# Layer 1's second-half output projection on the MLP's PSUM ring, with eight load buffers for its mixed tiles

## The chip, the cores and the metric

One core of one Trainium2 chip runs the whole program, once per launch. The time is device time in microseconds, from one launch; smaller is better. The core has five instruction queues that matter here: TensorE (PE; its weight loads are listed as PEld), VectorE (DVE), ScalarE (ACT), GpSimd (POOL) and SyncE (SP), which issues the DMA transfers. Each queue works its instructions off in order. SBUF and PSUM have 128 partitions; PSUM has eight banks, each of 512 float32 values a partition.

## What is computed

A trunk of two layers on a sequence of 1024 tokens with 1024 features, in float32. Layer 0 mixes with a convolution and attention on a memory, layer 1 with three kinds of attention. Both end in the same way, and only this end of layer 1 matters here:

```python
def squared_relu_mlp(h, w_in, w_out):
    return jnp.square(jax.nn.relu(h @ w_in)) @ w_out

# in each layer l, after the mixing
x = x + mix @ w_out[l]                                   # w_out: 1024 x 1024
x = x + squared_relu_mlp(rms_norm(x, norm_mlp_g[l]), w_mlp_in[l], w_mlp_out[l])   # 1024 x 4096 x 1024
```

## The kernel before

Features lie on partitions and tokens in columns. The sequence is worked in two halves of 512 tokens, so that a tile is 128 features by 512 tokens; x, the mixed activations (`act`) and the output of a half are eight such tiles each (`KT` = 8). To keep float32 accuracy each operand is split into a high and a low part (`split`: ACT copies the high part, L88, DVE takes the difference, L89), and each product is three matmuls: high by high, high by low, low by high. A weight tile (`weight`, L101 to L110) is loaded by SP into a buffer tagged `raw` (L106), copied by ACT (L109) and its difference taken (L110) into a buffer tagged `hl`; for half 1's output projection L110 is on DVE, for the MLP on POOL.

The end of layer 1 is written at L1288 to L1302. `load_mix` (L376 to L381) loads the eight mixed tiles of a half from DRAM scratch (`mixd`, to which the attention has stored them) and splits them into `act`. `w_out` (L384 to L411) is the output projection: four pairs of output tiles (`ps_wo`), for each tile eight weight pieces of 128 x 128, held in two weight tiles, 48 matmuls a pair, 192 in all (L400 to L402); each finished tile is added to the residual (L404), squared on ACT, and added up in `acc` (L140). Then `act` is overwritten by x times the norm's gain, split again (L409, L410). `inv_rms` (L414 to L422) sums the squares over partitions (L150), makes the inverse root with small DVE operations, spreads it over all partitions with one more matmul (L164) and copies it with ACT to the tile `r` (L420). `mlp` (L424 to L473) does 16 rounds of an input projection of two tiles (`ps_i`, L441 to L443; scaled by `r` in L449, squared, split) and an output projection of eight tiles (`ps_mo`, L81 to L83), each of which is added to x by DVE (L463). The last round of a half stores x to the output (L1301 before the change, L1302 behind it).

Half 0 of this end (weights `k`, PSUM pool `ps2` with two banks) is written ahead of half 1 (context `ka`), but the order on the engines is made by a scheduler, which takes the instructions by priority and by when buffers come free: half 0's MLP runs in between the attention of half 1, and half 1's output projection follows on its last round. Buffers are given out by tag from pools; a tag with n buffers is a ring of n. A pool opened on the place of a closed one gives its first tile only when the readers of the old tiles there are done.

In the lines that the change touches, half 1's projection has a PSUM pool of its own, `psb`, with four banks (tag `a`), closed behind it; `ps3`, with four banks (tag `mm`), is opened when the MLP of half 1 is written, and stands on the same banks. The eight mixed tiles are loaded into the tag `raw`, three buffers (`NRAWA`), which also takes the weights.

Of the kernel before, what the change touches and what calls it, by code (L numbers as in the profile page):

```python
# [21 lines left out]
MIXORD = (4, 5, 6, 7, 0, 1, 2, 3)  # L22
# [64 lines left out]
def split(nc, hi, lo, src, eng=None):  # L87
    return (nc.scalar.activation(hi, src, AF.Copy),  # L88
            (eng or nc.vector).tensor_tensor(lo, src, hi.bitcast(F32), op=ALU.subtract))  # L89
# [286 lines left out]
def load_mix(k, act, src, kts, pool, tag="raw", bufs=2):  # L376

    for kt in kts:
        raw = pool.tile([P, HF], F32, tag=tag, name="mix", bufs=bufs)
        k.nc.sync.dma_start(raw, src[:, kt])  # L380
        split(k.nc, act[kt][:, 0], act[kt][:, 1], raw)  # L381


def w_out(k, l, mix, x, resid):  # L384


    nc = k.nc
    acc = k.tmp.tile([P, HF], F32, tag="acc", name="acc", bufs=2)
    for o in range(0, KT, WG):
        rs, ps = [], []  # L390
        for i in range(WG):
            rs.append(k.tmp.tile([P, HF], F32, tag="a", name="rs", bufs=2))
            nc.sync.dma_start(rs[i], resid[:, o + i])
            ps.append(k.psum.tile([P, HF], F32, tag=k.tag, name="ps_wo", bufs=k.nps))
        for g, kts in ((1, MIXORD[:4]), (0, MIXORD[4:])):
            w = [weights(k, k.i["w_out"][l, o + i][:, 512 * g:512 * g + 512], P) for i in range(WG)]
            for kt in kts:
                for i in range(WG):
                    wh, wl = (w[i][kt % 4][:, x] for x in range(2))
                    nc.tensor.matmul(ps[i], lhsT=wh, rhs=mix[kt][:, 0], start=kt == MIXORD[0], stop=False)  # L400
                    nc.tensor.matmul(ps[i], lhsT=wh, rhs=mix[kt][:, 1], start=False, stop=False)
                    nc.tensor.matmul(ps[i], lhsT=wl, rhs=mix[kt][:, 0], start=False, stop=kt == MIXORD[-1])  # L402
        for i in range(WG):
            nc.vector.tensor_add(x[o + i], ps[i], rs[i])  # L404
            sq_add(k, acc, x[o + i], o + i == 0, nc.vector if o + i > 5 else None)
        k.pe(24 * WG * HF / 2.4)
    for o in range(KT):
        a, g = mix[MIXORD[o]], k.cols[:, (C_MLP0, C_MLP1)[l] + o:][:, 0:1]
        nc.scalar.activation(a[:, 0], x[o], AF.Copy, scale=g)  # L409
        nc.vector.scalar_tensor_tensor(a[:, 1], x[o], g, a[:, 0].bitcast(F32), op0=ALU.mult, op1=ALU.subtract)  # L410
    return inv_rms(k, acc)  # L411
# [716 lines left out]
def build(tc, ins, out):  # L1128
    nc = tc.nc
    k = K()  # L1130
# [3 lines left out]
    def pool(es, name, side="left"):  # L1134
        return es.enter_context(tc.tile_pool(name=name, bufs=1, side=side))

    def psum_pool(name):
        return tc.tile_pool(name=name, bufs=1, space=bass.MemoryType.PSUM)

    with ExitStack() as es:  # L1140
# [15 lines left out]
        mixd = dram.tile([2, P, KT, HF], F32, name="mixd")  # L1156
# [10 lines left out]
        def act_tiles(hf):  # L1167
            return [ap.tile([P, 2, HF], F32R, tag=f"act{hf}{kt}", name=f"act{hf}{kt}", bufs=1) for kt in range(KT)]

        act = [act_tiles(hf) for hf in range(2)]  # L1170
# [72 lines left out]
        ka = K()  # L1243
# [44 lines left out]
        act = [act_tiles(hf) for hf in range(2)]  # L1288
# [1 line left out]
        load_mix(k, act[0], mixd[0], MIXORD, k.wpool, "raw", k.nraw)  # L1290
        rs = [w_out(k, 1, act[0], x[0], xs[0])]
        ka.rpool = pool(es, "rb", "right")
        with psum_pool("psb") as psb, tc.tile_pool(name="wb", bufs=1, side="right") as wb:
            ka.psum, ka.wpool, ka.tmp = psb, wb, wb
            load_mix(ka, act[1], mixd[1], MIXORD, ka.wpool, "raw", ka.nraw)
            rs.append(iter(list(w_out(ka, 1, act[1], x[1], xs[1]))))
        for hf in range(2):
            if hf == 1:
                k.psum = es.enter_context(psum_pool("ps3"))
                k.nps = 4  # L1300
            mlp(k, 1, x[hf], act[hf], rs[hf], lambda o: nc.sync.dma_start(out[hf, :, o], x[hf][o]))  # L1301
        k.flush()  # L1302

# [67 lines left out]
```

## Time and profile before

| what | us |
|---|---|
| median of 3 runs | 2467.85 |
| the runs | 2460.43, 2467.85, 2468.43 |
| the profiled execution, its time | 2460.16 |
| its span, from the first to the last instruction | 2458.4 |
| TensorE busy in the span | 2366.0 |
| last round of half 0's MLP ends, projection of half 1 starts | 2035.15, 2042.74 |
| projection ends, MLP of half 1 starts | 2090.07, 2100.68 |

The profile is of one execution. A timeline row gives the start, the time taken, the engine, line and operation, the tiles written and read, the count, and in brackets how long the engine was idle before it and what ended that. Matmuls overlap, so that the start of the next one, not the time of one, tells their pace.

### The profile page before, as it was taken

The numbers are of one execution on the slowest core, as the hardware profiler recorded it, in microseconds if no ns is written. First come the engines' busy times: TensorE is split into PE (matmuls) and PEld (weight loads), VectorE is DVE, ScalarE is ACT, GpSimd is POOL, SyncE is SP. The second block draws the span as 40 slices with busy tenths as digits, with TensorE's granted clock in tenths as the row PEclk, the third lists the DMA queues.
The fourth block names the chain that finished last, engine by engine and source line by source line (L and its number), as shares of the span: only waits on it lengthen the run. The fifth ranks groups of instructions, "written<-read, shape, count | busy, mean of one in ns | idle before, by whom it ended". The sixth has DMA issues, their size and how long they took to land.

```text
span 2458.4 us, 36789 instructions
## 1 busy us (share of the span) xinstructions
PE 2366.0 (96%) x12098; PEld 1995.2 (81%) x12098; DVE 1674.5 (68%) x3594; ACT 1293.9 (53%) x2938; POOL 1227.3 (50%) x1056
## 2 busy tenths in 40 slices
PE   7997999999988999999999999999999998899999
PEld 5786788888777988888887798888888886788887
DVE  7898587998678677877446866778777764333433
ACT  6565555333545467776334545676666653333332
POOL 2776643545633256565445325666565542344443
PEclk9998999999999999999999999999999999899999
DMA  6311433332444242322335434222221225233333
GB/s 215 100 48 57 137 103 102 96 98 91 138 124 150 83 124 82 87 86 83 116 103 170 149 99 131 80 70 66 76 86 59 70 75 178 65 98 95 95 95 103
DMA packets 157790, 250.87 MB, mean 102 GB/s; under 512 B 17696, under 2 KB 49056, under 8 KB 157088
## 3 DMA queue, kind: packets, MB, share of 16 engines
q1 hardware_dynamic: 157600, 248.52, 32.8%
q8 instruction: 96, 1.57, 0.3%
q14 instruction: 94, 0.77, 0.1%
HBM read 217.52 MB, written 20.45 MB: 97 GB/s over the span
## 4 chain that ended last, share of the span: by engine, by line
PE 63%; DVE 4%; DMA 2%; issue 2%; POOL 1%; ACT 1%; SPq 0%; ACTq 0%; POOLq 0%; DVEq 0%
PE ps_i L441 7%; PE ps_i L443 7%; PE ps_i L442 7%; PE ps_mo L81 6%; PE ps_mo L83 6%; PE ps_mo L82 6%; PE ps_t L1033 4%; PE ps_s L989 4%; PE ps_o L1049 2%; PE ps_o L1052 2%; PE ps_tok L666 1%; PE ps_tok L667 1%; PE ps_tok L668 1%; PE ps_wo L400 1%; PE ps_wo L402 1%
## 5 line engine op out<-in xcount | busy, mean ns | idle before, releaser
L110 POOL TENSOR_TENSOR hl<-raw,hl 128x512 fp32r<-128x512 f32 x592 | 773.1, 1317 | 867.0 <-ACT hl L109 827.8
L109 ACT ACTIVATE hl<-raw 128x512 fp32r<-128x512 f32 x656 | 409.7, 630 | 631.1 <-PE ps_i L443 261.3
L463 DVE TENSOR_TENSOR x<-x,ps_mo 128x512 f32<-128x512 f32 x512 | 348.3, 683 | 137.8 <-PE ps_mo L83 134.4
L441 PE MATMUL ps_i<-act,hl 128*128 128x512 f32 x1024 | 407.7, 398 | 8.9 <-DVE x L404 6.9
L81 PE MATMUL ps_mo<-hid,hl 128*128 128x512 f32 x1024 | 409.1, 400 | 5.9 <-DVE x L463 5.9
L443 PE MATMUL ps_i<-act,hl 128*128 128x512 f32 x1024 | 405.8, 396 | 0.0
L442 PE MATMUL ps_i<-act,hl 128*128 128x512 f32 x1024 | 404.0, 395 | 1.2 <-DVE act L410 1.2
L83 PE MATMUL ps_mo<-hid,hl 128*128 128x512 f32 x1024 | 401.2, 392 | 0.0
L82 PE MATMUL ps_mo<-hid,hl 128*128 128x512 f32 x1024 | 400.9, 392 | 0.0
L441 PEld LDWEIGHTS ps_i<-act,hl 128*128 128x128 f32 x1024 | 193.8, 189 | 51.4 <-DVE x L404 7.3
L449 DVE SCALAR_TENSOR_TENSOR a<-ps_i,r 128x512 f32<-128x512 f32 x128 | 88.0, 689 | 214.2 <-PE ps_i L443 207.2
L81 PEld LDWEIGHTS ps_mo<-hid,hl 128*128 128x128 f32 x1024 | 192.3, 188 | 48.0 <-DVE x L463 11.2
L442 PEld LDWEIGHTS ps_i<-act,hl 128*128 128x128 f32 x1024 | 193.7, 189 | 42.1 <-DVE act L410 2.2
L443 PEld LDWEIGHTS ps_i<-act,hl 128*128 128x128 f32 x1024 | 193.4, 189 | 41.7 <-issue 0.2
L83 PEld LDWEIGHTS ps_mo<-hid,hl 128*128 128x128 f32 x1024 | 192.3, 188 | 41.0
L82 PEld LDWEIGHTS ps_mo<-hid,hl 128*128 128x128 f32 x1024 | 192.7, 188 | 37.1 <-issue 0.5
L1000 ACT ACTIVATE prob<-ps_s,small 128x512 f32<-128x512 f32 (+3 forms) x240 | 141.1, 590 | 83.7 <-DVE small L998 53.4
L1019 POOL TENSOR_TENSOR prob<-prob,small 128x1024 f32<-128x1024 f32 (+3 forms) x120 | 180.0, 1525 | 1.2 <-DVE small L1013 0.6
L1041 DVE TENSOR_TENSOR PT<-ps_t,PT 128x512 fp32r<-128x512 f32 (+1 forms) x220 | 147.0, 671 | 48.2 <-ACT PT L1037 46.6
L1037 ACT ACTIVATE PT<-ps_t 128x512 fp32r<-128x512 f32 (+1 forms) x256 | 142.2, 566 | 60.0 <-PE ps_t L1033 56.4
L989 PE MATMUL ps_s<-KS,Q 128*128 128x512 f32 (+5 forms) x552 | 143.0, 358 | 0.0
L89 DVE TENSOR_TENSOR hid<-a,hid 128x512 fp32r<-128x512 f32 x128 | 100.7, 788 | 58.8 <-ACT hid L88 58.2
(292 smaller groups left out, 4716.0 us busy)
## 6 DMA issues: line engine op xcount, KB each, us to landing
raw<-in_w_mlp_in_dram SPq DMA_DIRECT2D x256, 256.0 KB, 2.7
raw<-in_w_mlp_out_dram SPq DMA_DIRECT2D x256, 256.0 KB, 2.9
raw<-in_w_out_dram SPq DMA_DIRECT2D x64, 256.0 KB, 3.1
Q<-Q SPq DMA_DIRECT2D x160, 64.0 KB, 2.0
raw<-in_cmp_w_dram SPq DMA_DIRECT2D x32, 256.0 KB, 2.7
raw<-in_a_w_dram SPq DMA_DIRECT2D x24, 256.0 KB, 2.8
raw<-in_b_wq_dram SPq DMA_DIRECT2D x24, 256.0 KB, 2.7
mixd<-ev SPq DMA_DIRECT2D x80, 64.0 KB, 2.1
```

Source lines behind the costliest of these rows:

```text
L81: nc.tensor.matmul(ps, lhsT=lh, rhs=rh, start=(i == 0), stop=False)
L82: nc.tensor.matmul(ps, lhsT=lh, rhs=rl, start=False, stop=False)
L83: nc.tensor.matmul(ps, lhsT=ll, rhs=rh, start=False, stop=(i == n - 1))
L109: nc.scalar.activation(hl[:, 0, :n], raw[:, :n], AF.Copy)
L110: k.last_lo = k.lo_eng.tensor_tensor(hl[:, 1, :n], raw[:, :n], hl[:, 0, :n].bitcast(F32), op=ALU.subtract)
L441: nc.tensor.matmul(p_, lhsT=wh, rhs=h[kt][:, 0], start=kt == 0, stop=False)
L442: nc.tensor.matmul(p_, lhsT=wh, rhs=h[kt][:, 1], start=False, stop=False)
L443: nc.tensor.matmul(p_, lhsT=wl, rhs=h[kt][:, 0], start=False, stop=kt == KT - 1)
L463: nc.vector.tensor_add(x[o], x[o], ps)
L989: nc.tensor.matmul(o_, lhsT=lhs, rhs=rhs, start=(n_ == 0), stop=(n_ == len(mms) - 1))
L1019: nc.gpsimd.tensor_tensor(t, t, sc[:, :, None].to_broadcast([P, 2, t.shape[-1]]), op=ALU.mult)
L1041: nc.vector.tensor_sub(PT[:, 1, :m], Tv[:, :m], PT[:, 0, :m].bitcast(F32))
```

## The change

Half 1's projection takes its PSUM tiles from `ps3`, which is now opened ahead of it, under the tag `mm`, the ring that the MLP of half 1 then goes on with. Its eight mixed tiles are loaded under a tag of their own, `mix`, with eight buffers, instead of under `raw`. The DMA scratch is set to 1024 bytes, which leaves more SBUF to the pools.

```diff
         rs = [w_out(k, 1, act[0], x[0], xs[0])]
         ka.rpool = pool(es, "rb", "right")
-        with psum_pool("psb") as psb, tc.tile_pool(name="wb", bufs=1, side="right") as wb:
-            ka.psum, ka.wpool, ka.tmp = psb, wb, wb
-            load_mix(ka, act[1], mixd[1], MIXORD, ka.wpool, "raw", ka.nraw)
+
+        ps3 = es.enter_context(psum_pool("ps3"))
+        with tc.tile_pool(name="wb", bufs=1, side="right") as wb:
+            ka.psum, ka.wpool, ka.tmp, ka.tag = ps3, wb, wb, "mm"
+            load_mix(ka, act[1], mixd[1], MIXORD, ka.wpool, "mix", 8)
             rs.append(iter(list(w_out(ka, 1, act[1], x[1], xs[1]))))
         for hf in range(2):
             if hf == 1:
-                k.psum = es.enter_context(psum_pool("ps3"))
-                k.nps = 4
+                k.psum, k.nps = ps3, 4
             mlp(k, 1, x[hf], act[hf], rs[hf], lambda o: nc.sync.dma_start(out[hf, :, o], x[hf][o]))
 ...
-    nc = bacc.Bacc("TRN2", target_bir_lowering=False, num_devices=1)
+    nc = bacc.Bacc("TRN2", target_bir_lowering=False, num_devices=1, dynamic_dma_scratch_size=1024)
```

The order changes only between the last store of mixed columns and the first input projection of half 1's MLP. On SP, the rows right behind that store (`mixd<-ev`) are these before; `mix` are the mixed tiles, `rs` the residual tiles, `out_dram` the stores of half 0's result, `raw` the weights of the matrix named:

```order
L380 DMA mix<-mixd 128x512 x3
L393 DMA rs<-xs 128x512 x2
L1301 DMA out_dram<-x_18496 128x512 x2
L380 DMA mix<-mixd 128x512
L106 DMA raw<-in_w_mlp_in_dram 128x512
L1301 DMA out_dram<-x_18497 128x512
L380 DMA mix<-mixd 128x512 x2
L106 DMA raw<-in_w_mlp_in_dram 128x512
L1301 DMA out_dram<-x_18497 128x512
L1301 DMA out_dram<-x_18498 128x512
L106 DMA raw<-in_w_mlp_in_dram 128x512
L1301 DMA out_dram<-x_18498 128x512
```

Behind these come a mixed tile, a store, an MLP weight, the last mixed tile, a store, and then the first output weight, the 23rd transfer. With the change the same place reads:

```order
L380 DMA mix<-mixd 128x512 x8
L393 DMA rs<-xs 128x512 x2
L106 DMA raw<-in_w_out_dram 128x512 x3
L1302 DMA out_dram<-x_18496 128x512 x2
L1302 DMA out_dram<-x_18497 128x512 x2
L1302 DMA out_dram<-x_18498 128x512
L106 DMA raw<-in_w_mlp_in_dram 128x512 x2
L1302 DMA out_dram<-x_18498 128x512
L106 DMA raw<-in_w_mlp_in_dram 128x512
L1302 DMA out_dram<-x_18499 128x512
L106 DMA raw<-in_w_out_dram 128x512 x2
```

All mixed tiles, the two residual tiles and three output weights stand first; the fourth output weight is the 24th transfer.

On DVE, in the last round of half 0's MLP, the differences of the mixed tiles (`act<-mix`) stand among the additions of half 0 (`x<-x,ps_mo`). Before:

```order
L89 TENSOR_TENSOR act_18494<-mix,act_18494 128x512
L463 TENSOR_TENSOR x_18497<-x_18497,ps_mo 128x512
L463 TENSOR_TENSOR x_18498<-x_18498,ps_mo 128x512 x2
L89 TENSOR_TENSOR act_18495<-mix,act_18495 128x512
L463 TENSOR_TENSOR x_18499<-x_18499,ps_mo 128x512
L89 TENSOR_TENSOR act_18488<-mix,act_18488 128x512
L463 TENSOR_TENSOR x_18499<-x_18499,ps_mo 128x512
L89 TENSOR_TENSOR act_18489<-mix,act_18489 128x512
L89 TENSOR_TENSOR act_18490<-mix,act_18490 128x512
L89 TENSOR_TENSOR act_18491<-mix,act_18491 128x512
L110 TENSOR_TENSOR hl<-raw,hl 128x512 x6
```

With the change:

```order
L89 TENSOR_TENSOR act_18494<-mix,act_18494 128x512
L463 TENSOR_TENSOR x_18497<-x_18497,ps_mo 128x512
L89 TENSOR_TENSOR act_18495<-mix,act_18495 128x512
L463 TENSOR_TENSOR x_18498<-x_18498,ps_mo 128x512
L89 TENSOR_TENSOR act_18488<-mix,act_18488 128x512
L89 TENSOR_TENSOR act_18489<-mix,act_18489 128x512
L89 TENSOR_TENSOR act_18490<-mix,act_18490 128x512
L463 TENSOR_TENSOR x_18498<-x_18498,ps_mo 128x512
L89 TENSOR_TENSOR act_18491<-mix,act_18491 128x512
L463 TENSOR_TENSOR x_18499<-x_18499,ps_mo 128x512
L110 TENSOR_TENSOR hl<-raw,hl 128x512 x2
L463 TENSOR_TENSOR x_18499<-x_18499,ps_mo 128x512
```

The differences of the fourth to seventh mixed tile (`act_18495` to `act_18490`) now stand ahead of the second addition into `x_18498`; with two banks in `ps2`, that addition frees the bank of half 0's last output tile.

On TensorE, at the end of half 1's projection, the difference of the two orders is this (- before, + with the change), `ps_n` being the norm's bank and `ps_i` the MLP's first tiles:

```order
 L402 MATMUL ps_wo<-act_18491,hl 128x512
 L150 MATMUL ps_n<-ones,acc 128x1 x4
-L164 MATMUL ps_n<-diag,ones 128x512
 L441 MATMUL ps_i<-act_18492,hl 128x512
 L442 MATMUL ps_i<-act_18492,hl 128x512
@@ -9211,4 +9210,5 @@
 L441 MATMUL ps_i<-act_18488,hl 128x512
 L442 MATMUL ps_i<-act_18488,hl 128x512
+L164 MATMUL ps_n<-diag,ones 128x512
 L443 MATMUL ps_i<-act_18488,hl 128x512
 L441 MATMUL ps_i<-act_18488,hl 128x512
```

The matmul that spreads the norm moves from ahead of the MLP's first matmul to behind its 26th. From the end of that tile pair on, the orders of TensorE and POOL are the same, and those of the other engines from the next weights on.

## Rows read from the trace of the kernel before

**Rows 1.** The page: span, busy time of the engines, and the data queue.
```profile
span 2458.4 us, 36789 instructions
PE 2366.0 (96%) x12098; PEld 1995.2 (81%) x12098; DVE 1674.5 (68%) x3594; ACT 1293.9 (53%) x2938; POOL 1227.3 (50%) x1056
...
q1 hardware_dynamic: 157600, 248.52, 32.8%
```

**Rows 2.** Chain of waits, half 0 to half 1: start, time taken, what.
```profile
2022.76 0.33 SPq L380
...
2023.61 5.15 DMA mix<-mixd
2028.78 0.64 ACT act L88
2029.44 0.69 DVE act L89
...
2037.29 4.74 DMA raw<-in_w_out_dram
2042.05 0.64 ACT hl L109
```

**Rows 3.** Timeline of TensorE, 2030 to 2048.
```profile
2030.79 0.50 PE L81 MATMUL ps_mo<-hid,hl 128*128 128x512 f32 x1 [1.26 <-DVE x L463]
...
2034.76 0.39 PE L83 MATMUL ps_mo<-hid,hl 128*128 128x512 f32 x1
...
2042.74 0.79 PE L400 MATMUL ps_wo<-act,hl 128*128 128x512 f32 x1 [7.59 <-ACT hl L109]
...
2048.02 0.44 PE L400 MATMUL ps_wo<-act,hl 128*128 128x512 f32 x1
```

**Rows 4.** Timelines of SP's issues and of ACT in that stretch.
```profile
2022.76 1.27 SPq L380 DMA_DIRECT2D mix<-mixd  x3
2024.08 0.91 SPq L393 DMA_DIRECT2D rs<-xs  x2
2025.08 0.85 SPq L1301 DMA_DIRECT2D out_dram<-x  x2
...
2025.80 0.63 ACT L88 ACTIVATE act<-mix 128x512 fp32r<-128x512 f32 x1 [4.00 <-DMA mix<-mixd]
```

**Rows 5.** Windows: length, busy time by engine, PEclk, DMA share, GB/s.
```profile
2025.00:2030.00 5.00, 3.18 (x13) 1.99 (x11) 2.45 (x4) 2.41 (x4) 0.00 (x0) 1.00 0.98 318
2030.00:2035.00 5.00, 4.21 (x18) 3.30 (x18) 3.35 (x7) 1.95 (x4) 2.48 (x2) 1.00 1.04 383
...
2037.00:2038.00 1.00, 0.00 (x0) 0.00 (x0) 0.00 (x0) 0.35 (x1) 0.96 (x1) 0.94 1.02 391
...
2048.00:2049.00 1.00, 1.00 (x5) 0.80 (x4) 0.00 (x0) 0.00 (x0) 0.00 (x0) 0.94 0.85 225
```

**Rows 6.** Projection to MLP: timeline of TensorE, then one window.
```profile
2088.67 0.40 PE L400 MATMUL ps_wo<-act,hl 128*128 128x512 f32 x1
...
2089.84 0.40 PE L402 MATMUL ps_wo<-act,hl 128*128 128x512 f32 x1
2093.09 1.87 PE L150 MATMUL ps_n<-ones,acc 128*128 128x1 f32 x8 [2.86 <-DVE acc L140]
2097.91 2.08 PE L164 MATMUL ps_n<-diag,ones 128*128 128x512 f32 x2 [2.95 <-DVE diag L156]
2100.68 0.79 PE L441 MATMUL ps_i<-act,hl 128*128 128x512 f32 x1 [0.69 <-ACT r L420]
...
2106.00:2107.00 1.00, 1.00 (x6) 0.83 (x5) 0.00 (x0) 0.00 (x0) 0.00 (x0) 0.93 0.00 0
```

**Rows 7.** Timeline of TensorE in layer 0, norm's broadcast inside the MLP.
```profile
315.42 0.39 PE L442 MATMUL ps_i<-act,hl 128*128 128x512 f32 x1
315.64 1.02 PE L164 MATMUL ps_n<-diag,ones 128*128 128x512 f32 x2
...
316.73 0.39 PE L441 MATMUL ps_i<-act,hl 128*128 128x512 f32 x1
```

## Prediction

> **What bounds the kernel now.** I read the page's busy shares first: TensorE is busy for 2366.0 us of a 2458.4 us span [rows 1], so the change can only win by closing a hole in TensorE's row or by sparing it time at the half clock. Both the program order and the diff point to one place, the hand-over from half 0 to half 1 in layer 1, so next I read the chain of waits and TensorE's timeline there. They show two holes.
>
> The first lies ahead of half 1's output projection. The last matmul of half 0's MLP starts at 2034.76 and ends at 2035.15; the projection's first matmul starts at 2042.74, after 7.59 us idle behind ACT [rows 3]. The chain says why: the last store of mixed columns lands, SP issues three mixed tiles at 2022.76, the fourth of them has to wait for a buffer, stores and MLP weights slip in between, and the first output weight is issued only at 2037.29, lands 4.74 us later and is copied by ACT at 2042.05 [rows 2]. In this stretch the DMA engines are full (share 0.98 and 1.04, 318 and 383 GB/s) [rows 5]: transfers are the scarce thing, and their order decides. The idle time also costs clock: the granted clock is 1.00 (2.4 GHz) while TensorE works, falls during the idle time (0.94 for the microsecond from 2037), is half (1.2 GHz) at the restart and is back in 2048 (0.94) [rows 5]. The first 12 matmuls take from 2042.74 to 2048.02 [rows 3].
>
> The second hole lies behind the projection. Its last matmul starts at 2089.84; the sums of squares wait for DVE's last addition until 2093.09 and run for 1.87 us; the broadcast of the norm waits for DVE until 2097.91; the MLP's first matmul waits for ACT's copy of that broadcast and starts at 2100.68 [rows 6]. It doesn't need the norm, which scales its result later: it needs a PSUM bank, and the pool that gives it (ps3) stands on the banks of the closed pool psb, whose last reader is that copy. The clock, idle times again behind it, is half until 2106.14 (0.93 for the microsecond from 2106) [rows 6].
>
> **Part 1: eight load buffers.** No instruction is added or removed. The room (8 tiles of 2 KB a partition) comes from the DMA scratch, which nothing here uses, since all data moves over the hardware queue [rows 1]; I cost that at nothing. What moves is SP's order: the eight mixed tiles, two residual tiles and three output weights now come first, and half 0's stores and the MLP's weights behind. The first output weight becomes the 11th transfer after the last mixed store instead of the 23rd.
>
> The pace: every transfer is 256 KB. Before, the first mixed tile was there at 2025.80 [rows 4] and the 23rd transfer at 2042.05 - about 22 steps in 16.25 us, 0.74 us each, reads and writes together. Reads alone may be slower: from 2025 to 2030, when few stores were under way, 262144 B at 318 GB/s [rows 5] are 0.82 us. The third mixed tile came two steps behind the first in 2.98 us (2025.80 to 2028.78), 1.49 us a step, with others served between [rows 2, 4]. As slow end for this burst I take 0.93 us, a little above the 0.82 that was measured over many transfers; 1.49 is kept for the rivals.
>
> The seventh mixed tile: 2025.80 + 6 x 0.74 = 2030.2, slow 2031.4. DVE takes its difference (L89) ahead of the addition that frees the PSUM bank for half 0's last output tile. Before, the same chain of landing, ACT copy, difference, addition and first matmul went from 2028.78 to 2030.79, 2.0 us [rows 2, 3]; the six matmuls of a tile take about 1.5 us. So half 0's last matmul ends at 2033.7, slow 2034.9. The first output weight: 2025.80 + 10 x 0.74 = 2033.2, slow 2035.1; from its landing to the matmul 2042.74 - 2042.05 = 0.69 us [rows 2, 3]: 2033.9, slow 2035.8. I take 2035.0 for the start of the projection, between the two, because more reads stand together than before. **Gain 7.7 us** (6.5 to 8.8).
>
> Clock: TensorE then waits only in pieces of 1 to 2 us, as in the 1.26 us of before [rows 3], during which the clock stayed at 1.00 [rows 5]. So the 12 matmuls run at full rate: a step is then 0.234 us (five from 2088.67 to 2089.84 [rows 6]), 2.8 us instead of 5.28. **Gain 2.5 us** (0 if the clock falls after all).
>
> What is late next: the fourth output weight. Its buffer is the first one's, so it stands 24th in SP's queue behind stores and MLP weights, and ACT copies it behind three MLP weights. It lands at 2025.80 + 23 x 0.74 = 2042.8, is usable at 2043.5, and TensorE wants it after 36 matmuls, 2035.0 + 8.4 = 2043.4. So they just meet: I allow 0.5 us of waiting, and 1.0 us because DVE now makes its low part behind the addition of the first finished projection tile (an operation of that size is 0.69 us [rows 2]). **Loss 1.5 us** (0 to 5.5: at 0.93 us a step it lands at 2047.2, 4.5 us late). Queued behind it on ACT and DVE are only later weights of the same projection. Sum of part 1: 7.7 + 2.5 - 1.5 = 8.7 us.
>
> Do queued transfers come in turn? The third mixed tile landed at 2028.78 [rows 2], 1.5 us after its turn at 0.74 a step (2027.3), with residual tiles and stores issued after it already being served [rows 4]. The Trainium skill (DMA: Bandwidth & Descriptors, Queues, rings and completion order) says that each DMA engine takes descriptors in the order of its ring. By that rule the projection would start at the quick end, 2033.9, but the fourth weight could not come before its turn either, and TensorE would wait 1.2 us for it: the sum would be 14.0 instead of 13.6 us, and the row of the third tile is against it.
>
> **Part 2: one PSUM ring.** Now half 1's projection, its norm and its MLP take banks in turn from ps3, so the MLP's first tile gets a bank freed long ago. In TensorE's order the broadcast moves from ahead of the MLP's first matmul to behind its 26th. The sums still stand first and still wait for DVE. So the MLP starts when they end, 2093.09 + 1.87 = 2094.96 in the old times, instead of 2100.68: 5.7 us. The broadcast now costs its own time in the stream. Layer 0 shows that arrangement: with it between two matmuls, their starts are 316.73 - 315.42 = 1.31 us apart instead of 2 x 0.23 with one matmul between, so 0.85 us at full clock [rows 7]. Before, the half clock went on for 5.4 us of the MLP (2100.68 to 2106.14); I let it go on as long from the new start, so the broadcast, 26 matmuls in, falls in full clock. **Gain 5.7 - 0.85 = 4.9 us.** Lower bound: the clock returns at the old moment; then 11.2 us at half hold the broadcast (1.7 us) and 21.6 matmuls of 0.44 us (5.28 / 12), against 12.4 done by then before; 9.2 x 0.234 = 2.2 us. Upper bound: the clock returns earlier by the 1.87 us of the sums, which saves 1.87 x (1 - 0.234 / 0.44) = 0.9: 5.8 us. Who waits for the norm: DVE's first scaling, which needs the whole 48-matmul pair and so comes some 5 us after the broadcast; on ACT two weight copies stand ahead of the norm's copy, 0.63 us each, and they wait for TensorE rows ahead of the broadcast: hidden.
>
> From there all orders are as before and TensorE is full; the gain stays to the end. Sum: 8.7 + 4.9 = 13.6 us. Span 2458.4 - 13.6 = 2444.8, that execution 2460.2 - 13.6 = 2446.6. It lies at the low end of the runs, which go from 2460.43 to 2468.43; I forecast against their median: 2467.85 - 13.6 = 2454.
>
> **The rivals.**
> - *The burst delays TensorE early.* Eight tiles share the engines, the first ones land late, DVE's differences hold up half 0's last additions, TensorE idles, its clock falls as it did in 2037, and the projection starts at 2038 at half: 4.7 + 0 - 1.5 + 4.9 = 8.1 us, 2459.7. For: a full DMA share. Against: only three tiles were in flight when the first one landed, and they still are the first three. Chance 0.14.
> - *The gain returns at weight four.* It comes 4.5 us late and the clock falls: 13.6 - 4.0 - 2.5 = 7.1 us, 2460.8. 0.14.
> - *The change doesn't do what it says*: the mixed tiles land no sooner for being issued sooner, so part 1 is nothing, part 2 its low end: 2.2 us, 2465.6. 0.05.
> - *Slower.* Weight four behind the longer queue: if the 24 transfers go at the 1.49 us per step of the third tile, it lands at 2060.1 and is used at 2060.8, 17.4 us late where I allowed 0.5; with 2.5 us of clock: 13.6 - 16.9 - 2.5 = -5.8 us, 2473.7. It decides from about 1.25 us a step. Against: 22 steps went at 0.74. 0.05.
>
> **How the numbers follow.** Forecast 0.62, the rivals 0.38 as above. Predicted 2454. Low end: the lowest run of before, 2460.4, less 16 (the upper bounds of both parts, less some waiting), 2444; high end: the highest, 2468.4, less 5.5, 2463; that leaves out the last two rivals and tails of the others. A difference of 0.3% (7.4 us) is what a measurement can tell: faster takes the forecast and about half of the first two rivals, 0.75; slower 0.05; same 0.20.
>
> **What would show it.** After: the idle time ahead of the projection's first matmul falls from 7.59 to under 2 us and its clock is full; a short wait stands at the 37th matmul of the projection (if 3 us or more: second rival); the MLP's first matmul follows the sums at once, with the broadcast inside it at about 0.9 us; the MLP's stretch is otherwise as long as before. I am wrong if the projection starts after 2037 in the old times, if its stretch is longer than 47 us, or if the MLP still waits for the norm.

## The result and the profile after

The changed kernel takes 2450.08 us, median of 7 runs (2442.82 to 2454.64); the kernel before, run beside it, 2461.60 us, median of 7 (2458.72 to 2468.43). The ratio of the means is 0.9946, with a 95% interval from 0.9927 to 0.9965: 13.3 us less, 8.6 to 18.0; the medians lie 11.5 apart. Faster, as forecast; the forecast time was 2454.

The two profiled executions seem to say less: the spans are 2458.4 [rows 1] and 2452.8 us, 5.6 apart. The changed one starts late into the changed place, though. The last store of mixed columns (L1056) is the last instruction on SP ahead of it; up to there both programs have the same order. Timelines of SP around that store; columns are start, time taken, engine, line and operation, tiles, count. Before:

```profile
2020.61 0.59 SPq L1056 DMA_DIRECT2D mixd<-ev  x1
```

After:

```profile
2029.53 0.59 SPq L1056 DMA_DIRECT2D mixd<-ev  x1
2031.68 3.65 SPq L380 DMA_DIRECT2D mix<-mixd  x8
2035.37 1.08 SPq L393 DMA_DIRECT2D rs<-xs  x2
2036.49 2.15 SPq L106 DMA_DIRECT2D raw<-in_w_out_dram  x3
2039.00 3.57 SPq L1302 DMA_DIRECT2D out_dram<-x  x5
```

This execution was 8.92 us late before the change could act. Below, a repeat of each kernel shows that this belongs to the execution and not to the program. So all places are counted from here on **from the issue of that store**; a time in the old trace is 2020.61 more. From store to end the kernel before takes 2458.4 - 2020.61 = 437.8 us, the changed one 2452.8 - 2029.53 = 423.3: 14.5 less, where 13.6 were forecast.

The page shows that the work itself stayed (busy TensorE 2366.0 in [rows 1]):

```profile
span 2452.8 us, 36786 instructions
...
PE 2365.7 (96%) x12098; PEld 1995.1 (81%) x12098; DVE 1676.9 (68%) x3594; ACT 1294.4 (53%) x2938; POOL 1224.9 (50%) x1056
```

**First hole.** TensorE's timeline after, from half 0's last tiles into the projection; in brackets the idle time ahead and what ended it:

```profile
2036.90 0.50 PE L81 MATMUL ps_mo<-hid,hl 128*128 128x512 f32 x1 [1.47 <-DVE x L463]
...
2039.80 0.50 PE L81 MATMUL ps_mo<-hid,hl 128*128 128x512 f32 x1 [1.23 <-DVE x L463]
...
2043.40 0.50 PE L81 MATMUL ps_mo<-hid,hl 128*128 128x512 f32 x1 [0.59 <-DVE x L463]
...
2044.66 0.39 PE L83 MATMUL ps_mo<-hid,hl 128*128 128x512 f32 x1
2044.89 0.40 PE L400 MATMUL ps_wo<-act,hl 128*128 128x512 f32 x1
...
2054.01 0.39 PE L401 MATMUL ps_wo<-act,hl 128*128 128x512 f32 x1
2054.85 0.50 PE L402 MATMUL ps_wo<-act,hl 128*128 128x512 f32 x1 [0.45 <-DVE hl L110]
```

The 7.59 us ahead of the projection [rows 3] are gone: its first matmul follows half 0's last in 0.23 us, 15.4 us behind the store (22.1 before). In half 0's tail three waits for DVE's additions, 3.3 us together, have taken the place of two with 2.6 before, the 1.26 of [rows 3] and this one:

```profile
2027.86 0.50 PE L81 MATMUL ps_mo<-hid,hl 128*128 128x512 f32 x1 [1.34 <-DVE x L463]
```

Half 0's last matmul now starts 15.1 us behind the store, 1.0 later than before. Windows of the same stretch after; columns are the length, busy time of PE, PEld, DVE, ACT and POOL, PEclk, DMA share and GB/s:

```profile
2031.00:2036.00 5.00, 4.43 (x20) 3.35 (x18) 1.82 (x3) 1.17 (x2) 1.66 (x2) 1.00 0.66 202
2036.00:2041.00 5.00, 2.87 (x11) 2.08 (x12) 5.00 (x8) 4.32 (x8) 1.34 (x1) 1.00 1.01 341
2041.00:2046.00 5.00, 4.41 (x19) 3.30 (x19) 5.00 (x9) 1.90 (x3) 0.00 (x0) 1.00 1.06 392
2046.00:2051.00 5.00, 5.00 (x23) 3.99 (x23) 0.95 (x2) 1.90 (x3) 2.42 (x2) 1.00 1.05 399
```

The granted clock stays at 1.00 (2.4 GHz), where it fell before [rows 5]. DVE is busy for all of the ten microseconds from 2036: between a landed mixed tile and the start of the projection it has become the engine that is waited for. About 1.1 of these ten microseconds are one instruction that took longer: the third difference, with 1.79 us instead of 0.68 (1.15 in a second profile of this kernel). GpSimd had begun a weight's difference 0.10 us ahead of it; what the traces show of such pairs stands under the last heading. Timeline of both engines:

```profile
2037.26 1.34 POOL L110 TENSOR_TENSOR hl<-raw,hl 128x512 fp32r<-128x512 f32 x1 [4.60 <-ACT hl L109]
2037.36 1.79 DVE L89 TENSOR_TENSOR act<-mix,act 128x512 fp32r<-128x512 f32 x1
```

**Second hole.** TensorE's timeline after, projection to MLP, and below it windows of the same stretch:

```profile
2090.19 0.39 PE L402 MATMUL ps_wo<-act,hl 128*128 128x512 f32 x1
2093.45 1.87 PE L150 MATMUL ps_n<-ones,acc 128*128 128x1 f32 x8 [2.87 <-DVE acc L140]
2095.18 0.77 PE L441 MATMUL ps_i<-act,hl 128*128 128x512 f32 x1
...
2103.02 0.39 PE L442 MATMUL ps_i<-act,hl 128*128 128x512 f32 x1
2103.24 1.02 PE L164 MATMUL ps_n<-diag,ones 128*128 128x512 f32 x2
2103.70 0.79 PE L443 MATMUL ps_i<-act,hl 128*128 128x512 f32 x1
2104.33 0.39 PE L441 MATMUL ps_i<-act,hl 128*128 128x512 f32 x1
```

```profile
2093.00:2099.00 6.00, 5.55 (x17) 4.78 (x18) 3.54 (x14) 0.08 (x1) 0.00 (x0) 0.50 0.00 0
2099.00:2100.00 1.00, 1.00 (x4) 0.78 (x4) 0.00 (x0) 0.00 (x0) 0.00 (x0) 0.74 0.00 0
```

The MLP starts at the end of the sums (before, 5.7 us later [rows 6]), and the broadcast stands inside it. The 2.87 us for DVE and the half clock (0.50, 1.2 GHz) behind them are left.

### The profile page after: what moved, and what is told of

Its sections match the earlier page's. It is cut to its first block, busy times and chain, and to the rows that moved or that the text cites. A ratio compares the mean times of both kernels' runs of the same rounds, so it can differ in the third digit from the quotient of the medians.

```text
span 2452.8 us, 36786 instructions
## 1 busy us (share of the span) xinstructions
PE 2365.7 (96%) x12098; PEld 1995.1 (81%) x12098; DVE 1676.9 (68%) x3594; ACT 1294.4 (53%) x2938; POOL 1224.9 (50%) x1056
## 4 chain that ended last, share of the span: by engine, by line
PE 62%; DVE 4%; DMA 3%; issue 2%; ACT 1%; POOL 1%; SPq 0%; ACTq 0%; DVEq 0%; POOLq 0%
PE ps_i L441 7%; PE ps_i L443 7%; PE ps_i L442 7%; PE ps_mo L81 6%; PE ps_mo L83 6%; PE ps_mo L82 6%; PE ps_t L1033 4%; PE ps_s L989 4%; PE ps_o L1049 2%; PE ps_o L1052 2%; PE ps_tok L666 1%; PE ps_tok L668 1%; PE ps_tok L667 1%; PE ps_wo L400 1%; PE ps_wo L402 1%
## 5 line engine op out<-in xcount | busy, mean ns | idle before, releaser
L110 POOL TENSOR_TENSOR hl<-raw,hl 128x512 fp32r<-128x512 f32 x592 | 771.6, 1314 | 877.6 <-ACT hl L109 840.1
L89 DVE TENSOR_TENSOR hid<-a,hid 128x512 fp32r<-128x512 f32 x128 | 100.9, 789 | 59.0 <-ACT hid L88 58.4
```

The lines of the kernel that those rows point to most:

```text
L110: k.last_lo = k.lo_eng.tensor_tensor(hl[:, 1, :n], raw[:, :n], hl[:, 0, :n].bitcast(F32), op=ALU.subtract)
```

## The experiments

Each kernel was timed beside the kernel before and profiled once, the kernel before and the changed one twice. The ratios come from several groups of runs, in which the median of the kernel before went from 2460.8 to 2464.4, so two kernels of different groups are compared through their ratios alone. The times of one kernel differ by 10 us between executions, so each profile is read in two stretches: from the last mixed store to the start of the projection's last matmul (part 1 acts there), and from that matmul to the span's end (part 2). "Pool" is half 1's projection with a PSUM pool of its own.

| kernel | store to last ps_wo | last ps_wo to end | store to end | ratio to before, interval |
|---|---|---|---|---|
| before | 69.2 | 368.6 | 437.8 | 1 |
| before, repeated | 69.7 | 367.9 | 437.5 | |
| scratch only | 68.5 | 367.5 | 436.0 | 0.9999 (0.9988 to 1.0011) |
| ring only | 70.0 | 362.8 | 432.8 | 0.9972 (0.9961 to 0.9982) |
| buffers only | 60.1 | 366.9 | 426.9 | 0.9959 (0.9946 to 0.9972) |
| after | 60.7 | 362.6 | 423.3 | 0.9946 (0.9927 to 0.9965) |
| after, repeated | 60.5 | 362.7 | 423.2 | |
| after, differences on GpSimd | 61.8 | 361.4 | 423.1 | 0.9941 (0.9926 to 0.9956) |
| after, three buffers | 58.6 | 361.4 | 420.0 | 0.9945 (0.9928 to 0.9961) |
| after, norm inside the MLP | 59.9 | 356.8 | 416.6 | 0.9927 (0.9915 to 0.9939) |
| norm inside, three buffers | 58.6 | 356.7 | 415.2 | 0.9908 (0.9893 to 0.9924) |
| norm inside, five buffers | 58.8 | 356.7 | 415.5 | 0.9913 (0.9894 to 0.9932) |

**Is the late start the execution's?** The same programs once more.

> The kernel before once more, for a second profile. The changed kernel's profiled execution was 8.9 us later than the first one of before already at the last mixed store, ahead of which the two programs have the same order. If that is a matter of the execution, the second profile puts the store anywhere between 2018 and 2032 us, while the stretch from the store to the end stays at 437.8 us within 1.5. If it belongs to the kernel, the store stands at 2020.6 within 1.

> The changed kernel once more, for a second profile. If the early 8.9 us are a matter of the execution, the store of the second profile stands elsewhere (2018 to 2032 us) and the stretch from the store to the end stays at 423.3 us within 1.5; if the change costs them, the store stands at 2029.5 within 1 again.

The store of the repeated kernel before stands at 2021.27, within 1 us of its first profile, which both readings allow. That of the repeated changed kernel stands at 2023.26, 6.3 us earlier than in its first profile, and this decides; over the twelve profiles it stands from 2019.48 to 2029.53. The stretch behind it is 437.5 and 423.2 us, within 0.3 of the first profiles. So the 8.92 us are the execution's, and the stretch is what the change is worth.

**Part 1 alone.**

```diff
-            load_mix(ka, act[1], mixd[1], MIXORD, ka.wpool, "raw", ka.nraw)
+            load_mix(ka, act[1], mixd[1], MIXORD, ka.wpool, "mix", 8)
...
-    nc = bacc.Bacc("TRN2", target_bir_lowering=False, num_devices=1)
+    nc = bacc.Bacc("TRN2", target_bir_lowering=False, num_devices=1, dynamic_dma_scratch_size=1024)
```

> Part 1 alone: the eight load buffers and the small DMA scratch, with half 1's projection back in its own PSUM pool. Measured from the issue of the last store of mixed columns, where the change's place begins: before takes 437.8 us to the span's end, the changed kernel 423.3. The prediction's theory (two separate holes, each closed by its own part): the projection starts 15.4 us behind that store (before 22.1), its last matmul some 60.7 (before 69.2), the 7.6 us from the sums of squares to the MLP's first matmul stay, and the end comes 429.2 us behind the store, 8.6 less than before (7.5 to 9.5). Rival, the two parts lean on each other (with its own pool the MLP's first matmul, or its weights, fall behind again): the hole ahead of the MLP grows from 7.6 to 10 us or more, and the end comes after 431.5. Ratio to before: 0.9965 by the theory.

The projection starts 14.8 us behind the store, with its last matmul at 60.1: 9.2 us earlier than before. The second hole is as it was, in TensorE's timeline:

```profile
2083.78 1.05 PE L150 MATMUL ps_n<-ones,acc 128*128 128x1 f32 x8 [2.87 <-DVE acc L140]
...
2087.78 2.07 PE L164 MATMUL ps_n<-diag,ones 128*128 128x512 f32 x2 [2.95 <-DVE diag L156]
2090.54 0.79 PE L441 MATMUL ps_i<-act,hl 128*128 128x512 f32 x1 [0.69 <-ACT r L420]
```

The end, 426.9, is 2.3 us better than expected. 0.6 of that lie in the first stretch; the other 1.7 follow the projection, where nothing was changed against before: in this execution the sums ran 1.05 us instead of 1.87, which is 0.8 of it. The other 0.9 lie behind the MLP's first matmul, where the half clock lasted 4.5 us instead of 5.5 (worth about 0.5, at 0.44 us a matmul instead of 0.234); the rest stays open. The rival of a growing second hole falls.

**Part 2 alone.** The changed kernel with its mixed tiles in the weights' ring:

```diff
-            load_mix(ka, act[1], mixd[1], MIXORD, ka.wpool, "mix", 8)
+            load_mix(ka, act[1], mixd[1], MIXORD, ka.wpool, "raw", ka.nraw)
```

> Part 2 alone: half 1's projection on the MLP's PSUM ring, the small DMA scratch, but the mixed tiles loaded through the three buffers that the weights use, as before. The prediction's theory: the projection still starts 22.1 us behind the last mixed store at half clock and its last matmul stands at 69.2; the MLP's first matmul follows the sums of squares at once (1.9 us from the sums' start instead of 7.6), and the end comes 431.8 us behind the store, 6.0 less than before (5 to 6.5). Rival, the shared ring also speeds the projection's own output tiles, or the whole gain is the ring's: the last matmul of the projection comes before 66 and the end before 428. Rival, the ring is worth only what half clock leaves (the prediction's lower bound): 435.6. Ratio to before: 0.9976.

TensorE's timeline at both holes, and a window behind the first:

```profile
2043.88 0.80 PE L400 MATMUL ps_wo<-act,hl 128*128 128x512 f32 x1 [9.38 <-ACT hl L109]
...
2094.42 1.87 PE L150 MATMUL ps_n<-ones,acc 128*128 128x1 f32 x8 [2.86 <-DVE acc L140]
2096.16 0.77 PE L441 MATMUL ps_i<-act,hl 128*128 128x512 f32 x1
```

```profile
2046.00:2048.00 2.00, 2.00 (x6) 1.52 (x6) 1.22 (x2) 1.10 (x2) 0.00 (x0) 0.50 0.50 152
```

The first hole stands, with half clock behind it; the MLP follows the sums at once. The end comes 5.0 us earlier than before (6.0 expected): behind the projection's last matmul 5.7 are gained, and 0.8 are lost ahead of it. Half 0 ended 1.2 us earlier here than before, 12.95 us behind the store instead of 14.15, and the projection still started at 22.7: the hole only grew to 9.38 us. What starts the projection before the change is the output weight, not half 0.

**The scratch alone.**

> The kernel before with the DMA scratch set to 1024 bytes and nothing else changed. The prediction costed this at nothing: the end comes 437.8 us behind the last mixed store, within 0.5, the projection starts at 22.1 and the ratio is 1. Rival, the scratch or the place of the buffers in SBUF matters by itself (for instance for the pace of the transfers): the pace of the burst behind the store changes, the projection's start moves by over 1 us, or the time by over 0.3%.

The ratio is 0.9999; the projection starts at 22.4. The end, 436.0, is outside the half microsecond that I had allowed, which was too narrow: 0.7 of it fall ahead of the projection's end, 1.0 behind, of which 0.8 are the sums, 1.05 us again. One profile of a stretch is good for some 1 to 2 us here, not for less.

**What sets the projection's start now?** The differences of the mixed tiles go to GpSimd:

```diff
-def load_mix(k, act, src, kts, pool, tag="raw", bufs=2):
+def load_mix(k, act, src, kts, pool, tag="raw", bufs=2, eng=None):
...
-        split(k.nc, act[kt][:, 0], act[kt][:, 1], raw)
+        split(k.nc, act[kt][:, 0], act[kt][:, 1], raw, eng)
...
-            load_mix(ka, act[1], mixd[1], MIXORD, ka.wpool, "mix", 8)
+            load_mix(ka, act[1], mixd[1], MIXORD, ka.wpool, "mix", 8, nc.gpsimd)
```

> The changed kernel, with the differences of half 1's eight mixed tiles taken by GpSimd instead of by VectorE. In the changed kernel TensorE waits three times for VectorE's additions in half 0's last tiles (1.47, 1.23 and 0.59 us), since differences of mixed tiles that have only just landed stand ahead of those additions on VectorE. Prediction's theory (the landing of the mixed tiles, passed on through VectorE's order, sets the start of the projection, and the output weights come just in time): with the differences away from VectorE the additions run at once, half 0's last matmul comes 1.5 to 3 us earlier than 15.1 us behind the last mixed store, but the projection then waits for its first output weight or for the mixed parts from GpSimd, whose differences take 1.1 us or more instead of 0.69: it starts between 13.5 and 15.4 and the end comes 421.5 to 423.3 us behind the store. Rival, the additions wait for nothing but TensorE and the holes belong to the two PSUM banks: half 0's last matmul stays at 15 and nothing changes. Rival, GpSimd becomes the bound (it also splits the MLP's weights): the projection starts after 16.5 us.

Rows of DVE, POOL and TensorE in this kernel, each from its engine's timeline, and a window behind the projection's start:

```profile
2024.06 0.69 DVE L463 TENSOR_TENSOR x<-x,ps_mo 128x512 f32<-128x512 f32 x1 [0.67 <-PE ps_mo L83]
```

```profile
2030.39 7.10 POOL L89 TENSOR_TENSOR act<-mix,act 128x512 fp32r<-128x512 f32 x5
```

```profile
2030.44 0.39 PE L83 MATMUL ps_mo<-hid,hl 128*128 128x512 f32 x1
2033.62 0.50 PE L400 MATMUL ps_wo<-act,hl 128*128 128x512 f32 x1 [2.80 <-ACT hl L109]
```

```profile
2035.00:2037.00 2.00, 2.00 (x6) 1.54 (x6) 2.00 (x2) 0.00 (x0) 2.00 (x2) 0.50 1.05 403
```

The additions now wait for TensorE alone, and half 0's last matmul starts at 11.0 instead of 15.1, 4.2 us earlier (I had said 1.5 to 3). So it was DVE's order that held half 0. But the first output weight is not there yet: TensorE waits 2.80 us for its copy and starts at 14.1, only 1.2 earlier than the changed kernel. The projection loses this again. Behind the wait the clock fell to half (0.50 in the window from 2035), which the shorter waits of the changed kernel had not cost, and the wait for weight four's low part was 0.92 us instead of 0.45: the last matmul stands at 61.8, 1.1 later than in the changed kernel. The end, 423.1, is the same only since the sums ran 1.05 us here and what follows the projection was 1.2 shorter. Two chains of nearly one length lie on top of each other, DVE's and the weight's; taking away one shows the other.

**How many buffers?**

```diff
-            load_mix(ka, act[1], mixd[1], MIXORD, ka.wpool, "mix", 8)
+            load_mix(ka, act[1], mixd[1], MIXORD, ka.wpool, "mix", 3)
```

> The changed kernel with three buffers instead of eight in the mixed tiles' own ring: the ring is still not shared with the weights, but the fourth mixed tile must again wait until the first is copied and its difference taken. It tells apart whether the gain of part 1 comes from the number of buffers or from the separate ring. If the number matters (the prediction's wording: all reads first, stores and later weights behind): the fourth tile is issued some 4 us later, stores and MLP weights slip ahead again, the projection starts between 18 and 21 us behind the last mixed store (15.4 with eight, 22.1 before), partly at half clock, and the end comes 426 to 430 us behind the store. If the separate ring alone is enough (the output weights have buffers at once): the projection starts at 15.4 to 16.5 and the end comes by 424.5.

The reading by the number of buffers fails outright: three are not worse, and the stretch is 3.2 us shorter. The reading by the separate ring holds, with a start earlier than the 15.4 to 16.5 that I had given it. The times don't show the 3.2 us (ratio 0.9945 against 0.9946); they rest on the profiles. Timelines of SP and of TensorE:

```profile
2023.98 0.59 SPq L1056 DMA_DIRECT2D mixd<-ev  x1
2026.13 1.27 SPq L380 DMA_DIRECT2D mix<-mixd  x3
2027.45 0.91 SPq L393 DMA_DIRECT2D rs<-xs  x2
2028.40 0.90 SPq L106 DMA_DIRECT2D raw<-in_w_out_dram  x2
2030.53 0.33 SPq L380 DMA_DIRECT2D mix<-mixd  x1
```

```profile
2035.13 0.50 PE L400 MATMUL ps_wo<-act,hl 128*128 128x512 f32 x1
...
2035.70 0.40 PE L81 MATMUL ps_mo<-hid,hl 128*128 128x512 f32 x1
```

The first output weight is the 6th transfer behind the store, issued at 4.4 us (7.0 with eight buffers). The projection starts at 11.2, and its matmuls interleave with half 0's last tiles, the last of which starts at 20.8. So part 1 needs no eight buffers. What it needs is that the weights stop waiting for mixed tiles to be split, and a ring of their own does that. A shared ring with more than three buffers was not run, so that it would do the same is not ruled out. Of the 3.2 us, 2.1 lie ahead of the projection's end; the other 1.2 are behind it, where again the sums ran 1.05 us instead of 1.87 (0.8 of it).

**What is left of the second hole.** The steps of half 1's projection are handed to the MLP's first round, which issues them between its own matmuls, instead of being used up ahead of it:

```diff
-        with tc.tile_pool(name="wb", bufs=1, side="right") as wb:
-            ka.psum, ka.wpool, ka.tmp, ka.tag = ps3, wb, wb, "mm"
-            load_mix(ka, act[1], mixd[1], MIXORD, ka.wpool, "mix", 8)
-            rs.append(iter(list(w_out(ka, 1, act[1], x[1], xs[1]))))
+        wb = pool(es, "wb", "right")
+        ka.psum, ka.wpool, ka.tmp, ka.tag = ps3, wb, wb, "mm"
+        load_mix(ka, act[1], mixd[1], MIXORD, ka.wpool, "mix", 8)
+        rs.append(w_out(ka, 1, act[1], x[1], xs[1]))
```

> The changed kernel, with one thing more: half 1's projection yields its steps to the MLP's first round, so that the sums of squares and the broadcast of the norm both stand inside the MLP's stream of matmuls instead of ahead of it. If what is left of the second hole is only the order (the sums wait 2.87 us for DVE's last addition while TensorE has matmuls that need nothing of it), the MLP's first matmul follows the projection's last at once, TensorE's clock stays whole, and the gain over the changed kernel is 2.9 us of idle time, 1.0 us of sums at half clock and about 1.9 us of MLP matmuls at half clock: the end comes at about 417.5 us behind the last mixed store instead of 423.3. Rival: the MLP's first tiles need the last output tile's activations anyway, since the norm's gain is applied after the residual addition, and TensorE waits for those instead: the idle time moves to the first matmul on the last activation tile, and the end comes at 421 to 423. Ratio to before 0.9917 by the first, 0.993 to 0.994 by the second.

TensorE's timeline, and a window:

```profile
2085.64 0.40 PE L402 MATMUL ps_wo<-act,hl 128*128 128x512 f32 x1
2085.88 0.40 PE L441 MATMUL ps_i<-act,hl 128*128 128x512 f32 x1
...
2093.21 0.95 PE L150 MATMUL ps_n<-ones,acc 128*128 128x1 f32 x8
```

```profile
2090.00:2094.00 4.00, 4.00 (x23) 3.41 (x22) 0.00 (x0) 1.26 (x2) 2.40 (x2) 1.00 0.01 4
```

No idle time, clock 1.00 throughout; the sums stand some 30 matmuls into the MLP, by when DVE's addition is long done. The end comes at 416.6, 6.6 us earlier than after (5.8 expected), of which 5.8 lie behind the projection's last matmul. The rival falls: TensorE waits for no activation. The times point the same way (ratio 0.9927 against 0.9946), but the two intervals overlap; the 6.6 us rest on the stretch.

**Both together.** The kernel just shown, with 3 and with 5 in place of the 8 buffers.

> Both improvements over the changed kernel together: the norm inside the MLP's stream, and three buffers instead of eight for the mixed tiles. From the last mixed store to the end the changed kernel takes 423.3 us; the norm alone brought it to 416.6 (6.6 less), the three buffers alone to 420.0 (3.2 less). If the two act at different places, as the theory of two holes says, the gains add: 413.4 us (412.5 to 414.5), ratio to before 0.9912 to 0.992. Part of the 3.2 us of three buffers lay in a shorter stretch at half clock behind the projection (0.9 us from the sums to the MLP's first matmul instead of 1.7), which the other change takes away as well: by that the end comes at 414.2. Rival, with three buffers the late mixed tiles only hide behind the hole that the norm's place left: the sum is 416 or more and the three buffers bring nothing.

> The same with five buffers for the mixed tiles: five of them are issued first, the sixth before and the last two behind the first two output weights. What decides by the last runs is where the first output weights stand behind the mixed store on SP's queue (6th with three buffers, 9th with five, 11th with eight) and whether VectorE's differences hold half 0's additions. If the weights' place decides, the end lies between three and eight buffers, 414.5 to 416 us behind the store. Rival, the number of mixed tiles at hand decides (the projection needs all eight within its first two tiles): five is best, under 413.

415.2 us with three buffers, outside the 412.5 to 414.5 that I had given to full addition (413.4), and short of no gain at all (416.6): the three buffers bring 1.4 us here, no more than a profile tells apart. The projection's end is at 58.6 as with three buffers before; their gain of 2.1 ahead of it shrinks to 1.3, since with the norm inside and eight buffers it was at 59.9 already, instead of 60.7. What lay behind the projection was the clock of one execution. Five buffers give 415.5, as the weight's place says, but 0.3 us is less than a profile tells apart. The kernel with three buffers takes 2441.51 us, median of 4, ratio 0.9908 (0.9893 to 0.9924): its interval lies below that of the change (0.9927 to 0.9965), though by 0.0003 only and in another group of runs. The kernel with five takes the same, 2441.49, and neither is told apart from eight buffers with the norm inside (0.9915 to 0.9939).

## Why the prediction was right, and where it was off

**The two holes, and that they are separate.** Right. By the table, the stretch up to the projection's end is 69.2, 69.7, 68.5 and 70.0 us with the shared weight ring, and 60.7, 60.5 and 60.1 with eight buffers (same place of the norm): means 69.35 and 60.42, part 1 is worth 8.9 us (8.7 forecast). Behind the projection, the four kernels with a pool take 366.9 to 368.6, mean 367.7, and the five on the ring with the norm ahead 361.4 to 362.8, mean 362.2: part 2 is worth 5.5 us (4.9 forecast, 2.2 to 5.8). The sum is 14.4, against 13.6. That part 1 is met so closely is in part luck: between the first profiles of the two kernels the start of the projection gained 6.8 us where 7.7 were forecast, and the projection itself became 1.8 shorter where 1.0 was forecast (2.5 of clock less 1.5 for weight four).

**The pace of the transfers.** Right, to a tenth of a microsecond. ACT's rows in the changed kernel, from its timeline, start when their transfer lands: the first mixed tile, the first output weight, the fourth.

```profile
2034.83 1.83 ACT L88 ACTIVATE act<-mix 128x512 fp32r<-128x512 f32 x3 [4.12 <-DMA mix<-mixd]
...
2042.34 2.01 ACT L109 ACTIVATE hl<-raw 128x512 fp32r<-128x512 f32 x3 [1.37 <-DMA raw<-in_w_out_dram]
...
2051.90 1.38 ACT L109 ACTIVATE hl<-raw 128x512 fp32r<-128x512 f32 x2 [1.47 <-DMA raw<-in_w_out_dram]
```

Ten steps in 7.51 us and 23 in 17.07: 0.75 and 0.74 us a step, as before. Counted from the store, the 11th transfer was there at 12.8 (12.6 forecast at that pace) and the 24th at 22.4 (22.2). The slow ends, 0.93 and 1.49 us a step, did not come, and with them fell the rivals of the early burst, of weight four and of the slower kernel. The Trainium skill (DMA: Bandwidth & Descriptors, Queues, rings and completion order) says that each DMA engine takes descriptors in the order of its ring; these three landings, each at its turn, agree with it better than the one row from which I doubted it. That row didn't come again: ACT copied the first three mixed tiles in 1.83 us without a pause, so the third was there within 1.3 us of the first, where it had taken 2.98.

**The start of the projection.** 2035.0 forecast in old times, 2036.0 measured (2035.9, 2035.4 and 2035.2 in the other three kernels with eight buffers and the same engines). The size is nearly right, the reason is not. In the prediction's sum the output weight came last, usable at 2033.9 (slow 2035.8), with half 0's last matmul done just ahead of it, at 2033.7 (slow 2034.9). The weight kept its time: its copy began at 2042.34, which is 2033.4 in old times, and the 0.69 us from there to the matmul give 2034.1. Half 0 ended at 2036.1, later than its slow end. I had let one landing, copy, difference, addition and matmul follow each other in 2.0 us, as for a single tile. In fact DVE was busy without a break from 2036 to 2046, with eight differences among the additions, one of them beside GpSimd's, and the three waits of TensorE fall to it; with the differences on GpSimd half 0 ended 4.2 us earlier. The step "I take 2035.0, because more reads stand together" got its allowance for the wrong thing: the reads kept their pace, DVE did not. The slow end of that sum, 2035.8, leaves a gain of 6.9, not the 6.5 that stands there; the start gained 6.8.

**The clock of the projection.** Right: 1.00 in the four windows shown and on to 2092, and the first matmuls follow each other in 0.23 us where [rows 3] had 0.44.

**Weight four.** The mechanism was right, the term too large: 1.5 us were allowed, 0.5 for the landing and 1.0 for DVE's order. Its high part came in time. The wait is for the low part, which stands on DVE behind the addition of the first finished tile, as forecast, but the step there is 2054.85 - 2054.01 = 0.84 us instead of 0.23: 0.6 us.

**The MLP.** It starts with the end of the sums, as forecast. The broadcast costs 2104.33 - 2103.02 = 1.31 us in place of two steps of 0.23, the 0.85 us read from layer 0 [rows 7]. I had half clock last 5.4 us from the MLP's start, as before; it was back in 2099, some 4.3 us after 2095.18, so the term came out near its upper bound. That bound had the right reason, an earlier return of the clock where work follows the sums at once, but with the wrong size: 1.1 us earlier, where the bound had the 1.87 of the sums. The lower bound has the broadcast in the half clock behind 21.6 matmuls, though it stands behind the 26th; with 25.4 matmuls at half and the broadcast at 0.85 it comes to 2.2 all the same.

**The rest.** From the MLP's first matmul to the end, 357.6 us after and 357.7 before. The 0.85 us of the broadcast are in the first and not in the second; the shorter half clock pays for about 0.5 of them, and what pays for the rest is within what one profile tells apart.

**The time itself.** 2454 against 2450.08. The step that was off is the base: the median of three runs, 2467.85, which seven runs put at 2461.60, 6.25 lower; two of the three were the slowest of the seven. Against that base the forecast gain would have given 2448.0, 2.1 too low, so that the error of the base was partly made up for. The range, 2444 to 2463, holds the median, but it is wide: it would have held 2461.60, no gain at all, too. What bears the mechanism out is the two stretches, not the range.

**What the change is for.** The prediction read part 1 as "all reads first". The three-buffer kernel shows that it is narrower: the output weight must not queue for a buffer behind mixed tiles, whatever else of the reads comes late. That was in the profile before: SP issued the fourth mixed tile late because the ring was full, and the first output weight last of all [rows 2, 4].

## What to carry to other kernels

A ring that two streams share makes the later stream wait for the earlier one's consumers; giving each its own was enough here with three buffers, and more brought nothing. Then look which engine's order now holds the start. A pool opened on a closed pool's banks makes its first user wait for the last reader there; where that is a value wanted only later, share the ring, and better still issue that value's steps inside the next stage, so that neither the idle time nor the half clock behind it is paid. When executions differ by more than the change is worth, compare the stretch from the last common instruction, and repeat one profile to know how far it can be trusted.

## What the runs showed of the hardware

- The same idle time left two clocks. After 2.86 or 2.87 us of waiting, the sums of squares ran for 1.87 us in four profiles (before, after, its repeat, ring only) and for 1.05 us in five (the repeat of before, scratch only, buffers only, differences on GpSimd, three buffers). That moves the end by about a microsecond in programs that are alike there, and no part of the change decides it. With no idle time the sums took 0.95 us.
- With reads and stores under way together the DMA engines moved 392 and 399 GB/s (windows from 2041 and 2046), more than the 341 of the five microseconds before.
- The difference of a mixed tile took 0.69 us on DVE and, for five in a row on GpSimd, 7.10 / 5 = 1.42 us, waits included.
- A difference on DVE could be held up by GpSimd. In the changed kernel's first trace 35 of DVE's differences at L89 and L110 took over 1 us; all 35 began while GpSimd was in a TENSOR_TENSOR instruction, and ended 0.28 or 0.55 us behind it. Another 177 began under one too and took less than 1 us; what decides is not shown.
- Up to the same store twelve executions took from 2019.48 to 2029.53 us, two of the changed kernel alone 6.3 us apart; where in the chip that arises, no run here shows.
